# The small transfers of RWKV's block inverse issued on POOL's queue instead of SP's

## Chip, cores and metric

The kernel runs on one core of a Trainium2 chip. The core has five engines with a queue each: TensorE (PE, matrix products into PSUM), VectorE (DVE), ScalarE (ACT), GpSimd (POOL) and SyncE (SP, which only issues transfers). The metric is the device time in microseconds of one execution.

## What is computed

One layer of a hybrid decoder trunk over 512 tokens of width 1,024, in float32: RMSNorm, one input projection, three groups of mixing heads side by side, an output projection with a residual, a gated feed-forward block with a causal convolution, and a last RMSNorm. Cut to what matters:

```python
h = _rmsnorm(x, attn_norm[l])
proj = h @ w_in[l]
p_nsa, p_rw, p_moba = _split(proj, [N_IN_NSA, N_IN_RWKV, N_IN_MOBA])
o_nsa, o_rw, o_moba = ...      # sparse attention | RWKV-7 time mixing | block attention
x = x + concat([o_nsa, o_rw, o_moba]) @ w_out[l]
x = x + _conv_glu(_rmsnorm(x, ffn_norm[l]), ...)
```

The RWKV part is a recurrence over the tokens with a 64 x 64 state for each of four heads:

```python
def step(state, inp):
    r_t, w_t, k_t, v_t, kk_t, a_t = inp
    sa = einsum('bhvk,bhk->bhv', state, -kk_t)
    state = state * w_t[:, :, None, :] + sa[..., None] * (kk_t * a_t)[:, :, None, :] \
            + v_t[..., None] * k_t[:, :, None, :]
    return state, einsum('bhvk,bhk->bhv', state, r_t)
```

## The kernel before

The recurrence is not run token by token. `rw_pair(p, ...)` handles a pair of heads (p = 0, 1) in 8 chunks of 64 tokens. Within a chunk the steps depend on each other through a lower-triangular 64 x 64 matrix, of which the inverse is wanted. It is found in blocks of 16: the 16 x 16 blocks on the diagonal are inverted one by one by elimination, and the rest follows from products on PE (L563 to L575).

The diagonal blocks come out of PE with a token to each partition (`GA`, masked to `NM`, summed to `Nc` at L479: 128 partitions, 8 x 16 numbers each). The elimination on DVE (L491 to L496, fifteen steps of a product and a sum) wants a whole block within a partition (`NB` and `X`: 64 partitions, 256 numbers each). The data is therefore laid out anew through scratch tensors in DRAM, by six transfers of 64 KB for each pair of heads:

- L481 writes `Nc` to `s1`, L483 reads `s1` back as `NB`.
- After the elimination, L503 writes `X`, transposed (`XX`) and as it is, to an `s2` each, and L505 reads each back as `Xc` (named `Nc` in the profile, since it lies in that tile). L508 spreads them to the block-diagonal matrices `DvT` and `Dv`.

A read waits until its write has landed. DVE can't start the elimination before `NB` is there, nor `DvT` and `Dv` before the two reads; PE's L563 needs `DvT`, L571 and L573 need `Dv`. A `lock` lets the second pair start its inverse only after the first pair's.

Beside this run, at the same time, the projections (`proj_fm`, PE's L240 to L242) with weights that SP loads (`wload`, L217, six buffers `wraw`) and that ACT and DVE split into a high and a low part (`whi` L211, `wlo` L212), and the attention heads (`evac_q`: `P` L696, `qt` L701 and L702; scores L784). All of them are generators with hand-written costs that `merge()` interleaves; that gives the order in which instructions are written down. The tile framework then sorts each engine's queue by its own estimate of when an instruction is ready, gives out buffers and sets the semaphores; at run time each queue runs strictly in that order.

Before the change all loads and all these small transfers are issued by SP. POOL clears buffers (L201, L489, L490, L716, L890) and takes a few powers of small tiles (L293, L392, L673, L862, L1455).

Of the kernel before, what the change touches and what calls it, by code (L numbers as in the profile page):

```python
# [78 lines left out]
def cap(name):  # L79
    return CAPS.get(name, CDEF)  # L80
# [11 lines left out]
def hybrid_layer(ctx: ExitStack, tc: tile.TileContext, xT, cst, cols, lora, fgain, wA, wVn, cw1,  # L92
                 wO, wF, wG, out, dbg=None):
    nc = tc.nc
    act, dve, pool, pe, sp = nc.scalar, nc.vector, nc.gpsimd, nc.tensor, nc.sync
# [4 lines left out]
    def at(site):  # L100
        return pool if ENG[site] == 'p' else dve
# [245 lines left out]
    def rw_pair(p, r, k, v, L):  # L347
# [98 lines left out]
        for c0 in (0, 2):  # L446
            yield from want(2)
            pbs = rbank(), rbank()
            for cc in (c0, c0 + 1):
                for j, src in ((0, bb), (1, kb)):  # L450
                    o = ((cc - c0) * 2 + j) * 128
                    for par, cp in ((0, 0), (1, 1), (0, 1), (1, 0)):
                        (r0, r1), (q0, q1) = R64[par], R64[cp]
                        c = 2 * cc + cp
# [3 lines left out]
            for par in range(2):  # L458
                src = pbs[par].rearrange("p (k j a t) -> p a k j t", k=2, j=2, a=2)
# [18 lines left out]
        Nc = v8(NX, 0)  # L478
        dve.tensor_reduce(Nc, NM.rearrange("p (c b j) -> p c j b", b=4, j=16), axis=AX.X, op=OP.add)  # L479
        s1 = dr.tile([NCH, 128, 16], F32, name="s1", bufs=cap("s1"))  # L480
        sp.dma_start(s1.rearrange("c p j -> p c j"), Nc)  # L481
        NB = v16(BT, 0)
        sp.dma_start(NB, s1.rearrange("c (b i) j -> (c b) i j", b=8))  # L483
        for u in range(2):
            dve.tensor_tensor(ch(R)[:, 4 * u:4 * u + 4], GA[u][:, :, :, 0, :].rearrange("p k h t -> p (k h) t"),
                              con("offmask")[:, None, :].to_broadcast([128, 4, CH]), op=OP.mult)
# [13 lines left out]
        Dv, DvT = r2("Dv"), r2("DvT")  # L500
        for src, dst, eng in ((XX, DvT, dve), (X, Dv, at('dv'))):
            s2 = dr.tile([NCH, 128, 16], F32, name="s2", bufs=cap("s2"))
            sp.dma_start(s2.rearrange("c (b i) j -> (c b) i j", b=8), src)  # L503
            Xc = v8(NX, 1 + (src is X))
            sp.dma_start(Xc, s2.rearrange("c p j -> p c j"))  # L505
            for u in range(2):
                c4 = slice(4 * u, 4 * u + 4)
                eng.tensor_tensor(dst.rearrange("p (c b j) -> p c b j", b=4, j=16)[:, c4],  # L508
                                  Xc[:, c4, None, :].to_broadcast([128, 4, 4, 16]),
                                  bsel4, op=OP.mult)  # L510
            yield crw
# [135 lines left out]
        for cc in range(4):  # L647
            for par, cp in ((0, 0), (1, 1), (0, 1), (1, 0)):
                c = 2 * cc + cp
# [533 lines left out]
    def rw_run(p):  # L1183
        g = rw_pair(p, *(rin0 if p == 0 else [rin1[i] for i in (T_R, T_K, T_V)]), L)
        n = 0
        for dt in g:
            yield dt
            n += 1
            mark(f'RW{p}.{n:02d}')
# [362 lines left out]
```

## Time and profile before

| | us |
|---|---|
| three runs | 731.89, 730.33, 729.77 |
| median | 730.33 |
| the profiled execution | 731.48 |
| its span in the profile | 729.4 |

The span runs from the first to the last instruction of the program on the core; the profiled execution's own time has some 2 us around it. In the rows, L12 is line 12 of the kernel; an entry in square brackets is the idle time of the engine ahead of an instruction and what ended it.

### The profile page before, as it was taken

Reading aid. Unit: us, or ns where it says so; the run is one execution under the profiler, and the core shown is the slowest. Engines: PE = TensorE matmul, PEld = TensorE weight load, DVE = VectorE, ACT = ScalarE, POOL = GpSimd, SP = SyncE. Lnnn points to the kernel's source line nnn. Section 1 sums busy time; section 2 is a strip of 40 time slices with the busy share of each in tenths; the row PEclk is TensorE's granted clock in tenths of the full one; section 3 lists DMA queues with packets and bytes.
Section 4 is the critical chain, followed back from the end, with each engine's and each line's share of the span. In section 5 each row is a group of like instructions: output and inputs, shape, how many; then the busy total and the mean of one; then the engine's idle time right before and its main releaser. Section 6 shows DMA issues by size and latency. Waiting matters only on the chain. (4 is left out here: it accounts for less than half of the span.)

```text
span 729.4 us, 13565 instructions
## 1 busy us (share of the span) xinstructions
PE 705.4 (97%) x5156; PEld 613.6 (84%) x5156; DVE 627.0 (86%) x1377; ACT 415.3 (57%) x862; POOL 30.8 (4%) x46
## 2 busy tenths in 40 slices
PE   9999988899999999999999999999999999999995
PEld 6777867678788788888899899999999999998884
DVE  6579679878897999797999999999999999999804
ACT  8475434465656877774766546455564555657403
POOL 4010100000000000011000000000000000000001
PEclk9989989999999999999999999999999999999999
DMA  9622021513110022024246333323333333346003
GB/s 328 193 87 80 13 50 49 140 65 117 44 44 30 1 59 73 30 72 145 74 144 218 97 107 102 116 87 102 97 108 101 102 103 110 98 126 201 1 1 115
DMA packets 44800, 69.86 MB, mean 96 GB/s; under 512 B 10688, under 2 KB 12352, under 8 KB 44736
## 3 DMA queue, kind: packets, MB, share of 16 engines
q1 hardware_dynamic: 44016, 67.95, 29.4%
q10 hardware_dynamic: 720, 1.06, 0.4%
q8 instruction: 40, 0.66, 0.4%
q14 instruction: 24, 0.20, 0.1%
HBM read 64.40 MB, written 4.59 MB: 95 GB/s over the span
## 5 line engine op out<-in xcount | busy, mean ns | idle before, releaser
L1301 ACT CAST ah<-S 128x512 fp32r<-128x512 f32 x88 | 54.5, 621 | 57.6 <-DVE S L1296 57.6
L240 PE MATMUL mm<-xh,whi 128*128 128x512 f32 x152 | 69.6, 458 | 0.0
L241 PE MATMUL acc<-dn,dn 128*128 128x512 f32 (+1 forms) x173 | 64.3, 372 | 0.0
L242 PE MATMUL acc<-dn,dn 128*128 128x512 f32 (+1 forms) x173 | 63.8, 371 | 0.0
L242 PE MATMUL mm<-xh,wlo 128*128 128x512 f32 x152 | 61.8, 406 | 0.0
L241 PE MATMUL mm<-xl,whi 128*128 128x512 f32 x152 | 61.5, 404 | 0.0
L1302 DVE TENSOR_TENSOR al<-S,ah 128x512 fp32r<-128x512 f32 x88 | 58.7, 682 | 0.7 <-ACT ah L1301 0.6
L791 ACT ACTIVATE prob<-prob,fixed 128x128 f32<-128x128 f32 (+1 forms) x72 | 40.5, 563 | 28.5 <-DVE fixed L788 26.5
L240 PE MATMUL acc<-dn,dn 128*128 128x512 f32 (+1 forms) x173 | 54.9, 371 | 0.0
L211 ACT CAST whi<-wraw 128x512 fp32r<-128x512 f32 x70 | 42.6, 618 | 19.8 <-PE mm L241 14.1
L212 DVE TENSOR_TENSOR wlo<-wraw,whi 128x512 fp32r<-128x512 f32 x70 | 47.3, 682 | 3.6 <-PE mm L242 2.2
L240 PE MATMUL pB<-bh,ah 128*128 128x256 f32 x172 | 50.1, 291 | 0.1
L242 PE MATMUL pB<-bh,al 128*128 128x256 f32 x172 | 48.6, 283 | 1.1 <-DVE al L1302 1.0
L242 PE MATMUL pC<-bh,al 128*128 128x256 f32 x172 | 48.5, 282 | 0.3 <-DVE al L1302 0.3
L240 PE MATMUL pC<-bh,ah 128*128 128x256 f32 x172 | 48.5, 282 | 0.2 <-ACT ah L1301 0.2
L241 PE MATMUL pB<-bl,ah 128*128 128x256 f32 x172 | 48.3, 281 | 0.0
L241 PE MATMUL pC<-bl,ah 128*128 128x256 f32 x172 | 48.1, 280 | 0.0
L1302 DVE TENSOR_TENSOR al<-wraw,ah 128x512 fp32r<-128x512 f32 x66 | 43.4, 681 | 0.0
L823 ACT CAST ph<-pt 128x512 fp32r<-128x512 f32 (+3 forms) x72 | 29.7, 425 | 23.3 <-PE pt L816 22.4
L788 DVE CUSTOM_DVE_ANT_0 prob<-s,early 128x128 f32<-128x128 f32 (+1 forms) x72 | 34.7, 483 | 6.6 <-PE s L785 5.0
L1301 ACT CAST ah<-wraw 128x512 fp32r<-128x512 f32 x66 | 36.8, 618 | 1.4 <-DVE x L1135 1.3
L241 PEld LDWEIGHTS acc<-dn,dn 128*128 128x128 f32 x173 | 32.6, 188 | 5.3 <-DVE dn L1365 0.2
(400 smaller groups left out, 2211.8 us busy)
## 6 DMA issues: line engine op xcount, KB each, us to landing
wraw<-in_wF_dram SPq DMA_DIRECT2D x88, 256.0 KB, 2.7
wraw<-in_wG_dram SPq DMA_DIRECT2D x44, 256.0 KB, 3.0
wraw<-in_wA_dram SPq DMA_DIRECT2D x38, 256.0 KB, 3.0
xr<-in_xT_dram SPq DMA_DIRECT2D x16, 256.0 KB, 4.1
wraw<-in_cw_dram SPq DMA_DIRECT2D x16, 256.0 KB, 3.3
wraw<-in_wO_dram SPq DMA_DIRECT2D x16, 256.0 KB, 2.6
fraw<-in_wA_dram SPq DMA_DIRECT2D x8, 256.0 KB, 5.2
x2d<-x2o SPq DMA_DIRECT2D x8, 256.0 KB, 3.3
```

What stands on the lines that cost most here:

```text
L211: act.copy(hi[:, :w], raw)
L212: dve.tensor_tensor(lo[:, :w], raw, hi[:, :w].bitcast(F32), op=OP.subtract)
L240: pe.matmul(o, ah, bh, start=first, stop=False)
L241: pe.matmul(o, ah, bl, start=False, stop=False)
L242: pe.matmul(o, al, bh, start=False, stop=last)
L788: dve.tensor_tensor_reduce(out=P, in0=s_[:, 0:n], in1=con("cmask")[:, 512 - n:512], scale=1.0, scalar=3e38, op0=OP.add, op1=OP.min, accum_ ...
L791: act.activation(P, P, AF.Exp, bias=m, scale=-1.0, accum_out=sums[:, i, par:par + 1])
L823: act.copy(h, t_[:, 0:n])
L1301: act.copy(h, src)
L1302: at(f'L{i}').tensor_tensor(l, src, h.bitcast(F32), op=OP.subtract)
```

## The change

The six transfers of the inverse are issued by POOL (`nc.gpsimd`) instead of SP (`nc.sync`). They move the same bytes between the same places and wait for the same data. POOL has no other transfers.

```diff
@@ -478,9 +478,9 @@
         Nc = v8(NX, 0)
         dve.tensor_reduce(Nc, NM.rearrange("p (c b j) -> p c j b", b=4, j=16), axis=AX.X, op=OP.add)
         s1 = dr.tile([NCH, 128, 16], F32, name="s1", bufs=cap("s1"))
-        sp.dma_start(s1.rearrange("c p j -> p c j"), Nc)
+        pool.dma_start(s1.rearrange("c p j -> p c j"), Nc)
         NB = v16(BT, 0)
-        sp.dma_start(NB, s1.rearrange("c (b i) j -> (c b) i j", b=8))
+        pool.dma_start(NB, s1.rearrange("c (b i) j -> (c b) i j", b=8))
@@ -500,9 +500,9 @@
         Dv, DvT = r2("Dv"), r2("DvT")
         for src, dst, eng in ((XX, DvT, dve), (X, Dv, at('dv'))):
             s2 = dr.tile([NCH, 128, 16], F32, name="s2", bufs=cap("s2"))
-            sp.dma_start(s2.rearrange("c (b i) j -> (c b) i j", b=8), src)
+            pool.dma_start(s2.rearrange("c (b i) j -> (c b) i j", b=8), src)
             Xc = v8(NX, 1 + (src is X))
-            sp.dma_start(Xc, s2.rearrange("c p j -> p c j"))
+            pool.dma_start(Xc, s2.rearrange("c p j -> p c j"))
```

## Rows read from the trace of the kernel before

**Rows 1.** The page's engine totals: busy us, share of the span, instructions.
```profile
PE 705.4 (97%) x5156; PEld 613.6 (84%) x5156; DVE 627.0 (86%) x1377; ACT 415.3 (57%) x862; POOL 30.8 (4%) x46
```

**Rows 2.** Stretches: length, busy us (count) by engine, granted clock, DMA share, GB/s.
```profile
90.00:100.00 10.00, 6.66 (x46) 4.54 (x45) 6.74 (x16) 3.63 (x6) 0.00 (x0) 0.75 0.40 93
```

**Rows 3.** The transfers: packets, and issues with count, KB each, us to landing.
```profile
DMA packets 44800, 69.86 MB, mean 96 GB/s; under 512 B 10688, under 2 KB 12352, under 8 KB 44736
...
Nc<-s SPq DMA_DIRECT2D x4, 64.0 KB, 2.9
...
NB<-s SPq DMA_DIRECT2D x2, 64.0 KB, 2.3
```

**Rows 4.** SP's timeline, 55 to 145 us: start, length, transfer.
```profile
68.14 0.39 SPq L481 DMA_DIRECT2D s<-Nc  x1
...
85.54 1.09 SPq L503 DMA_DIRECT2D s<-X  x2
88.99 1.27 SPq L505 DMA_DIRECT2D Nc<-s  x2
...
110.21 0.47 SPq L483 DMA_DIRECT2D NB<-s  x1
```

**Rows 5.** SP's own waits, 50 to 150 us: total us, times, longest.
```profile
SPq L481 <- DVE Nc L479: 21.9, 2, 13.0
SPq L503 <- DVE X L498: 14.4, 1, 14.4
...
SPq L505 <- DMA s<-X: 3.1, 2, 2.3
```

**Rows 6.** DVE's timeline, 55 to 150 us, around both inverses.
```profile
73.05 0.18 DVE L494 TENSOR_TENSOR NB<-NB,X 64x15 f32<-64x15 f32 x1 [0.18 <-DMA NB<-s]
...
91.50 0.76 DVE L508 TENSOR_TENSOR DvT<-Nc,early 128x256 f32<-128x256 f32 x2 [4.78 <-DMA Nc<-s]
92.58 0.76 DVE L508 TENSOR_TENSOR Dv<-Nc,early 128x256 f32<-128x256 f32 x2 [0.32 <-DMA Nc<-s]
93.25 0.69 DVE L696 SCALAR_TENSOR_TENSOR P<-mm,early 128x512 f32<-128x512 f32 x1
...
114.49 0.17 DVE L494 TENSOR_TENSOR NB<-NB,X 64x15 f32<-64x15 f32 x1
...
140.49 0.76 DVE L508 TENSOR_TENSOR DvT<-Nc,early 128x256 f32<-128x256 f32 x2 [1.37 <-DMA Nc<-s]
```

**Rows 7.** PE's timeline, 84 to 112 us.
```profile
91.37 0.40 PE L242 MATMUL mm<-xh,wlo 128*128 128x512 f32 x1
...
95.91 0.47 PE L784 MATMUL s<-kk,qt 128*128 128x128 f32 x1 [3.34 <-DVE qt L702]
...
97.58 0.79 PE L240 MATMUL mm<-xh,whi 128*128 128x512 f32 x1
...
100.31 0.41 PE L784 MATMUL s<-kk,qt 128*128 128x256 f32 x1
...
105.47 0.39 PE L240 MATMUL mm<-xh,whi 128*128 128x512 f32 x1
...
106.86 0.39 PE L784 MATMUL s<-kk,qt 128*128 128x512 f32 x1
```

**Rows 8.** POOL's timeline, 0 to 260 us.
```profile
1.39 0.52 POOL L716 MEMSET kl<- 64x512 f32 x1
...
30.34 1.02 POOL L293 TENSOR_TENSOR early<-fixed 128x4 f32<-128x4 f32 x1 [11.57 <-DVE fixed L292]
44.87 2.03 POOL L392 TENSOR_TENSOR fixed<-fixed 128x8 f32<-128x8 f32 x1 [13.51 <-DVE fixed L389]
74.02 1.64 POOL L392 TENSOR_TENSOR fixed<-fixed 128x8 f32<-128x8 f32 x1 [27.12 <-DVE fixed L389]
```

**Rows 9.** Waits of PE's weight loads, 55 to 160 us.
```profile
PEld rw L533 <- DVE hl L942: 0.4, 1, 0.4
```

**Rows 10.** Readers and writers of `wraw`, 50 to 150 us: what ended their idle time.
```profile
  PE mm L241: 11.4, 5
```

## The prediction, made before the change was run

> **What bounds the kernel now.** Read the engine totals first [rows 1]: TensorE (PE) is busy for 705.4 of 729.4 us, so nearly every microsecond that PE is made to wait is a microsecond of time, and what PE does not wait for is free. VectorE (DVE) is second at 627.0 us; POOL does almost nothing, 30.8 us. Next, the table by stretches [rows 2]: both block inverses run between 67 and 142 us, and the worst ten microseconds for PE of the whole middle part lie there, 6.66 us busy between 90 and 100 us, with the granted clock at 0.75 on average, so in part at the lower of the two levels (1.2 GHz). Third, the two engines' own timelines. PE stands still for 3.34 us before L784 at 95.91 us, waiting for DVE's `qt` [rows 7]. Going back along DVE [rows 6]: `qt` needs `P` (L696, 93.25 us), which is behind the `Dv` products (92.58), which are behind `DvT` (91.50), which waited 4.78 us for the transfer `Nc<-s` of L505. So one transfer of the moved twelve already sits on the chain that stops PE. The second inverse has the same shape: `DvT` at 140.49 us after a wait of 1.37 us on `Nc<-s`, and a little later PE loads for L533 behind DVE's L942, itself behind `Dv`, after a wait of 0.4 us [rows 9].
>
> **What leaves SP.** Per pair SP issues six transfers: L481, L483, twice L503, twice L505. They cost about 0.4 to 0.5 us of SP each, as 0.39 for one L481 and 1.09 and 1.27 for two L503 and two L505 show [rows 4]; twelve are some 5 us. More time goes where SP stands at them: 21.9 us before L481, 14.4 before L503 [rows 5], and weight loads (L217) stand in line behind. Do the loads come late? In the group of waits on `wraw` from 50 to 150 us, the engines that read it sat idle 11.4 us, and what released them was above all PE (a buffer of the split weights), no transfer [rows 10]. An earlier weight load would land in a buffer that nobody yet wants. I cost the gain at nothing; the cover is the six `wraw` buffers, and if it went, a cast would wait for a landing, about 3 us as for `Nc` (2.9 [rows 3]).
>
> Do the twelve themselves wait behind weight loads on SP? No: SP stands ready at each and waits for what the transfer itself needs, DVE's `Nc` before L481, DVE's `X` before L503, the landed write before L505 (3.1 us) [rows 5]; then it starts them, at 68.14, 85.54 and 88.99 us [rows 4]. So there is no queueing to be saved.
>
> **What is added on POOL.** The shapes decide. L481 and L505 have one side in runs of 16 floats, 64 bytes, so 128x8 = 1,024 pieces for 64 KB; L483 and L503 move 64 runs of 1 KB. Six transfers of 1,024 pieces are 6,144 of the 10,688 packets under 512 B in [rows 3]. SP's landing times show little penalty (2.3 us for `NB`, 2.9 for `Nc` [rows 3]), but the trace holds no transfer issued by POOL. Its cost beyond SP's I bound from POOL's own rows [rows 8]. Low end: nothing, a queue like SP's. High end: POOL's two-operand instruction takes 1.02 us on 128x4 = 512 elements (L293) and 1.64 us on 1,024 (L392); the line through both is 0.40 us fixed and 1.24 us per 1,024. If POOL treats a piece as an element, a 64-piece transfer is later by 0.4 and a 1,024-piece one by 1.64 us. I take 0.4 and 1.0 us: nearer the high end than nothing, because a queue that builds 1,024 pieces in POOL is closer to the row with as many elements than to no work.
>
> The Trainium skill bears on this (DMA: Bandwidth & Descriptors, Specifications): the first byte takes about 1 us from GpSimd and 0.6 from SP or ACT, so 0.4 us per transfer; no row here shows it. By it alone the sum below would be four transfers x 0.4 for the first pair and two x 0.4 for the second, 2.4 us.
>
> **The sum, order of work unchanged.**
> - First pair, `NB`: write (1.0) and read (0.4) later. DVE waits 0.18 us for it at 73.05 already [rows 6], so no slack: +1.4 us, and DVE's chain of L494/L496 ends 1.4 later.
> - First pair, `DvT`/`Dv`: the write L503 +0.4, then two reads one behind the other on POOL, each +1.0, so the second lands 2.4 later. `P` stands behind `Dv`, so PE's gap grows from 3.34 by 1.4 + 2.4 = 3.8 us.
> - Second pair, `NB`: the read is issued at 110.21 and lands 2.3 us on [rows 3, 4], about 112.5; L494 runs at 114.49 [rows 6]. Slack 2.0 covers 1.4: nothing.
> - Second pair, `DvT`/`Dv`: DVE already waits, so +2.4 us, and PE's wait of 0.4 at L533 grows by as much.
> - POOL's other work: `X` of pair 1 is cleared long before it is read, and L392 at 74.02 would come after the read issued near 71: nothing, unless POOL's queue puts a waiting transfer ahead of L392, on whose result DVE's L398 waits next.
>
> Sum 3.8 + 2.4 = 6.2 us. With the high prices: 0.4 + 1.64 + 0.4 + 3.28 = 5.7 and 3.7, 9.4 us. A longer PE gap may also lengthen the slow spell: after the present gap six 128x512 matmuls take 2.73 us (97.58 to the L784 at 100.31), later six take 1.39 (105.47 to the L784 at 106.86) [rows 7], so one more spell costs about 1.3 us; I keep two of them in the upper bound, not in the sum. The profiled execution took 731.48 us (span 729.4 plus 2.1 outside), so it would become 737.7; the median of the runs is 730.33, so I predict 736.5 us. This case's own range is 732.5 (which is past the bound of a measurable change) to 742 (9.4 plus two spells).
>
> **Rivals.**
> - *The transfers are as quick and stay hidden.* POOL's queue could cost no more than SP's. For it: POOL is idle, and none of the four waits in [rows 6] is long but one. Against: DVE waits on three of the four without slack. Time 730.3, within 2.2 us of it (0.3%, about what a measurement of this kernel can tell from no change).
> - *Faster: the order of work changes.* The queues are not in line order: POOL clears `kl` of L716 at 1.39 us, long ahead of L293 [rows 8]. A planner sorts instructions by when it thinks they are ready. If it prices POOL's transfers so that `Nc<-s` comes later than the end of `P`'s matmuls (91.37 + 0.40, about 91.8 us [rows 7]), it will write `P` and `qt` ahead of `DvT`. Then `P` runs about 1.4 us earlier than 93.25, the slow spell (1.3) may go with the gap, and the second pair's wait of 1.37 is filled: -4.1 us, 726.2. It decides when `P` precedes `DvT` in DVE's queue and the later `DvT` is needed by nobody yet. Against: a planner that is off by the same 4.78 us today would have to be right.
> - *Much slower: POOL builds the pieces slowly.* If POOL builds the reading and the writing side of each piece in turn, a 1,024-piece transfer costs 2x1.64 = 3.28 us more. First pair 0.4 + 3.28 + 0.4 + 6.56 = 10.6; second pair 1.6 beyond the slack at `NB` and 7.0 at `Dv`; 19.2 us, 749.5. It becomes the case from about 2 us per transfer. For it: L392 took 2.03 us at 44.87 and 1.64 at 74.02 [rows 8], so POOL's work can be stretched. Against: that is 0.4 us, not a doubling. The Trainium skill has this as a rule against the change (SBUF — State Buffer, SBUF: two separate sides): while DVE runs in a mode that takes both ports, GpSimd can't write its transfer descriptors, and the advice is to issue from ACT or SP; no transfer in the trace of before can show it.
>
> **How the numbers follow.** Chances: order kept and stalls longer 0.43 (736.5); slow building 0.15 (749.5); hidden 0.19 (730.3); reordered for the better 0.23 (726.2). A part of the first case, 0.02, falls within 0.3%. So faster 0.23, same 0.21, slower 0.56. The range leaves out about half of the faster case and half of the slow one, together 0.19: 726.5 to 749 us. The likeliest case alone is 732.5 to 742.
>
> **What the profile after would show.** A new queue of transfers of POOL's, with 12 of 64 KB, and landings longer than 2.3 to 2.9 us: over 3.5 for the 1,024-piece ones if the sum is right, unchanged if they are hidden, over 5 if building is slow. DVE's wait before `DvT` above 4.78 us, `NB`'s above 0.18, and PE's gap before L784 near 7 us. SP no longer standing at L481 and L503, with its weight loads earlier and no cast the better for it. The prediction is wrong if POOL's landings equal SP's, if `P` stands ahead of `DvT`, or if the queues between 150 and 380 us, where PE still waits here and there, are sorted anew: that would move the time by an amount these rows can't price.

## The result, and the profile after

The changed kernel took 735.15 us (median of 6 runs, 734.32 to 737.39); the kernel before, timed beside it, 730.50 (729.77 to 731.89). The ratio is 1.0071, with a 95% interval of 1.0054 to 1.0087: slower by 4.65 us, in the direction of the forecast (736.5) and inside its range. The profiled execution has a span of 733.6 us where the one before had 729.4.

The page's engine totals, the line of packets and the new queue:

```profile
PE 703.9 (96%) x5156; PEld 612.3 (83%) x5156; DVE 627.2 (85%) x1377; ACT 415.7 (57%) x862; POOL 39.8 (5%) x58
...
DMA packets 38464, 69.86 MB, mean 95 GB/s; under 512 B 4544, under 2 KB 5824, under 8 KB 38400
...
q0 software_dynamic: 384, 0.79, 0.5%
...
q8 instruction: 40, 0.66, 0.4%
```

Against [rows 1], POOL has 12 more instructions and 9.0 us more busy time; PE's busy time is 1.5 us less, and the time is longer all the same, so what grew is PE's standing. Against [rows 3], 6,144 small packets are gone: the 12 transfers on POOL's queue make 384 packets, 32 each (the trace's packet records show 16 of 4 KB and 16 of 4 bytes).

The transfers' landings from the same execution (count, KB each, median us), and POOL's timeline, which answers to [rows 4] and [rows 8]:

```profile
s<-X POOLq DMA_DIRECT2D x4, 64.0 KB, 3.2
Nc<-s POOLq DMA_DIRECT2D x4, 64.0 KB, 3.8
...
s<-Nc POOLq DMA_DIRECT2D x2, 64.0 KB, 4.3
NB<-s POOLq DMA_DIRECT2D x2, 64.0 KB, 2.1
```

```profile
67.76 1.07 POOL L481 DMA_DIRECT2D s<-Nc  x1 [21.81 <-DVE Nc L479]
74.10 0.56 POOL L483 DMA_DIRECT2D NB<-s  x1 [5.27 <-ACT vn L747]
76.96 1.66 POOL L392 TENSOR_TENSOR fixed<-fixed 128x8 f32<-128x8 f32 x1 [2.31 <-DVE fixed L389]
88.99 1.12 POOL L503 DMA_DIRECT2D s<-X  x2 [10.37 <-DVE X L498]
91.24 0.93 POOL L505 DMA_DIRECT2D Nc<-s  x1 [1.13 <-DMA s<-X]
93.26 0.90 POOL L505 DMA_DIRECT2D Nc<-s  x1 [1.09 <-DMA s<-X]
...
109.65 0.89 POOL L481 DMA_DIRECT2D s<-Nc  x1 [15.00 <-DVE Nc L479]
112.96 0.55 POOL L483 DMA_DIRECT2D NB<-s  x1 [2.42 <-DMA s<-Nc]
```

The first `s<-Nc` was issued at 67.76 and landed 5.8 us later, the second in 2.8; the view of line L481 gives these two ends of the 4.3 in the list. (At 74.10 the view names ACT's `vn` as the releaser because it ended at about that time; L483 needs the landing.) POOL issues a transfer of 1,024 pieces in 0.9 to 1.07 us and one of 64 runs in 0.55, where SP took about 0.4 to 0.5 [rows 4].

POOL also starts later on what it has waited for. In the second pair the kernel before and then the changed one show:

```profile
106.92 1.03 DVE L479 TENSOR_REDUCE Nc<-NM 128x128 f32<-128x512 f32 x1
107.98 0.38 SPq L481 DMA_DIRECT2D s<-Nc  x1
```

```profile
108.33 1.03 DVE L479 TENSOR_REDUCE Nc<-NM 128x128 f32<-128x512 f32 x1
```

SP issued the write 0.03 us after `Nc` was ready and the read 0.06 after the write's landing; POOL (109.65 and 112.96 above) 0.30 and 0.54 after. From `Nc` to the landing of `NB` it was 4.43 us and is 5.64.

DVE's and PE's timelines and the stretches, against [rows 6], [rows 7] and [rows 2]:

```profile
76.20 0.18 DVE L494 TENSOR_TENSOR NB<-NB,X 64x15 f32<-64x15 f32 x1 [3.98 <-DMA NB<-s]
...
94.23 0.76 DVE L508 TENSOR_TENSOR DvT<-Nc,early 128x256 f32<-128x256 f32 x2 [4.33 <-DMA Nc<-s]
96.61 0.76 DVE L508 TENSOR_TENSOR Dv<-Nc,early 128x256 f32<-128x256 f32 x2 [1.62 <-DMA Nc<-s]
97.28 0.68 DVE L696 SCALAR_TENSOR_TENSOR P<-mm,early 128x512 f32<-128x512 f32 x1
...
144.32 0.76 DVE L508 TENSOR_TENSOR DvT<-Nc,early 128x256 f32<-128x256 f32 x2 [3.26 <-DMA Nc<-s]
145.97 0.76 DVE L508 TENSOR_TENSOR Dv<-Nc,early 128x256 f32<-128x256 f32 x2 [0.89 <-DMA Nc<-s]
```

```profile
76.93 0.39 PE L240 MATMUL mm<-vw,xh 128*128 128x274 f32 x1 [2.95 <-DVE fixed L389]
...
99.94 0.33 PE L784 MATMUL s<-kk,qt 128*128 128x128 f32 x1 [3.23 <-DVE qt L702]
...
100.89 0.50 PE L240 MATMUL mm<-xh,whi 128*128 128x512 f32 x1
...
102.39 0.28 PE L784 MATMUL s<-kk,qt 128*128 128x256 f32 x1
...
144.80 1.15 PE L533 MATMUL rw<-DvT,R 64*64 64x64 f32 x32 [0.90 <-DVE DvT L508]
146.99 0.50 PE L240 MATMUL mm<-xh,whi 128*128 128x512 f32 x1 [1.04 <-DVE Sall L628]
```

```profile
70.00:80.00 10.00, 7.05 (x50) 6.83 (x49) 4.30 (x17) 4.43 (x9) 2.21 (x2) 0.90 0.06 18
80.00:90.00 10.00, 10.00 (x69) 9.43 (x69) 9.52 (x36) 4.16 (x10) 1.01 (x2) 0.93 0.08 26
90.00:100.00 10.00, 6.76 (x72) 4.72 (x70) 4.09 (x9) 3.26 (x7) 2.37 (x5) 1.00 0.28 61
100.00:110.00 10.00, 10.00 (x135) 7.87 (x135) 8.14 (x23) 3.47 (x10) 0.35 (x1) 1.00 0.15 48
```

Three readings. First, PE now stands in two places of the first pair: a new gap of 2.95 us at 76.93, behind L389, which stands behind `NB` in DVE's queue; and the old one before L784, 3.23 us where it was 3.34. Second, in the second pair PE stands 0.90 and 1.04 us around L533, where [rows 9] had 0.4. Third, the granted clock: in the kernel before it was at its lower level behind the gap before L784 (0.75 in [rows 2]); now that stretch has 1.00, six matmuls there take 1.50 us (100.89 to 102.39) where they took 2.73 [rows 7], and the lower level (the trace's clock record puts it from 78.0 to 81.4) falls behind the new gap.

How far the work is behind, from the start times that the views of lines L481 (first and second pair's `s<-Nc`) and L673 (POOL, far behind both inverses) give, in single profiled executions:

```
us                                  L481 to L481    second L481 to L673
before                68.1  108.0   39.9            187.5   79.5
changed               67.8  109.7   41.9            191.0   81.3
L481/L483 on POOL     66.3  107.4   41.1            186.5   79.1
L503/L505 on POOL     66.1  107.0   40.9            188.4   81.4
on ACT's queue        67.0  103.7   36.7            184.3   80.6
SP, P first           67.2  102.8   35.6            182.1   79.3
POOL, P first         66.0  105.2   39.2            185.7   80.5
SP, L508 of pair 1 on POOL   65.6 100.2  34.6       179.7   79.5
SP, L508 of both on POOL     66.8 101.3  34.5       181.9   80.6
changed, packets moved       75.9 114.4  38.5       195.3   80.9
before, packets moved        75.8 112.8  37.0       192.4   79.6
```

The change costs 2.0 us in the first pair's stretch and 1.8 in the second's, 3.8 of the span's 4.2. The other rows are the experiments below.

### The profile page after: what moved, and what is told of

Read it like the earlier page. It is cut to its first block, busy times and chain, and to the rows that moved or that the text cites. A ratio compares the mean times of both kernels' runs of the same rounds, so it can differ in the third digit from the quotient of the medians.

```text
span 733.6 us, 13566 instructions
## 1 busy us (share of the span) xinstructions
PE 703.9 (96%) x5156; PEld 612.3 (83%) x5156; DVE 627.2 (85%) x1377; ACT 415.7 (57%) x862; POOL 39.8 (5%) x58
## 2 busy tenths in 40 slices
DMA packets 38464, 69.86 MB, mean 95 GB/s; under 512 B 4544, under 2 KB 5824, under 8 KB 38400
## 4 chain that ended last, share of the span: by engine, by line
PE 64%; DVE 8%; ACT 4%; issue 1%; DMA 1%; POOL 1%; SPq 0%; POOLq 0%; ACTq 0%
PE acc L241 5%; PE acc L242 5%; PE acc L240 5%; PE mm L240 4%; PE mm L242 4%; PE mm L241 4%; PE pB L240 3%; PE pB L242 3%; PE pB L241 2%; PE ot L804 2%; PE pC L240 2%; PE pC L241 2%; PE pA L241 2%; PE pC L242 2%; PE pA L240 2%; PE pA L242 2%
```

## The experiments

**Which half of the change costs what.** The write and read of `Nc` and `NB` alone on POOL (the lines shown), and, in a second kernel, those of `X` (L503, L505) alone:

```diff
-        sp.dma_start(s1.rearrange("c p j -> p c j"), Nc)
+        pool.dma_start(s1.rearrange("c p j -> p c j"), Nc)
...
-        sp.dma_start(NB, s1.rearrange("c (b i) j -> (c b) i j", b=8))
+        pool.dma_start(NB, s1.rearrange("c (b i) j -> (c b) i j", b=8))
```

> Only L481 and L483 go through POOL; the four transfers of the second half stay on SP. Theory (each longer round trip on POOL's queue stands on DVE's path to the next product, and the two halves add): the first pair's NB is about 3 us later than before, DVE waits some 4 us before L494 at 73 us, P and PE's L784 are about 3 us later; the second pair's NB has slack and costs nothing: 732.5 to 733.5 us against 730.5. Rival (the loss sits in the second half, L503 and L505, or in the sorting of DVE's queue around it): 730.5 within 1 us.

> Only L503 and L505 go through POOL; PE's, DVE's and ACT's queues are in the same order as before, so nothing but the path of the transfers differs. Theory: the second read lands later in both pairs, 1 to 2 us before Dv of the first pair and 2 to 3 us before Dv of the second: 732 to 733.5 us. Rival (the whole loss is the slow first write of the first half, 5.8 us to landing): 730.5 within 1 us. The gains of e1 and e2 over the kernel before should add up to the 4.6 us of the whole change, if nothing is given back.

Measured, with the kernel before at 729.28: 731.75 us, ratio 1.0034 (1.0011 to 1.0056), for the first; 731.46, ratio 1.0031 (1.0019 to 1.0044), for the second. Both times lie under their bands, while the increments, 2.5 and 2.2 us, are those expected (2 to 3 and 1.5 to 3). Their sum, 0.65%, is close to the whole, 0.71%: within these intervals the halves add up. The stretches say where each half costs: the first 1.2 us in the first pair and nothing in the second (39.9 to 41.1, 79.5 to 79.1), the second 1.0 and 1.9. DVE waited 3.10 us for `NB` in the first, where some 4 were expected, and its stretches, of an execution of 730.27 us, show less of the cost than its median does. With L503/L505 alone moved, DVE's timeline of the first pair shows where it waits:

```profile
90.69 0.76 DVE L508 TENSOR_TENSOR DvT<-Nc,early 128x256 f32<-128x256 f32 x2 [6.01 <-DMA Nc<-s]
91.61 0.76 DVE L508 TENSOR_TENSOR Dv<-Nc,early 128x256 f32<-128x256 f32 x2 [0.16 <-DMA Nc<-s]
92.29 0.68 DVE L696 SCALAR_TENSOR_TENSOR P<-mm,early 128x512 f32<-128x512 f32 x1
```

6.01 us against 4.78 [rows 6], and PE's gap before L784 was 4.37 us.

**Is it POOL, or leaving SP?** All twelve on ACT's queue (one of the four lines; the others alike):

```diff
-        sp.dma_start(s1.rearrange("c p j -> p c j"), Nc)
+        act.dma_start(s1.rearrange("c p j -> p c j"), Nc)
```

> All six transfers on ACT's queue, which is of the same kind as SP's, instead of POOL's. Theory (POOL's way of issuing costs, not leaving SP): landings of 2.2 to 3.5 us as on SP, no wait for NB beyond 0.5 us, 730 to 732 us, with whatever ACT loses while it stands at the transfers. Rival (taking them off SP costs or gains by itself, through the weight loads that move up): slower than 734, or faster than 729.

Measured: 727.92 us, ratio 0.9984 (0.9965 to 1.0003): under the 730 to 732 of its theory and past the rival's 729, so the expectation missed. DVE didn't wait for `NB`. With these transfers the planner wrote `P` ahead of `DvT`, the reordering that was a rival in the prediction:

```profile
89.56 0.69 DVE L696 SCALAR_TENSOR_TENSOR P<-mm,early 128x512 f32<-128x512 f32 x1 [2.15 <-PE mm L242]
...
91.25 0.76 DVE L508 TENSOR_TENSOR DvT<-Nc,early 128x256 f32<-128x256 f32 x2
93.47 0.76 DVE L508 TENSOR_TENSOR Dv<-Nc,early 128x256 f32<-128x256 f32 x2 [1.46 <-DMA Nc<-s]
94.27 1.41 DVE L702 TENSOR_TENSOR qt<-P,qt 64x512 fp32r<-64x512 f32 x2
```

PE's gap before L784 fell to 1.72 us. ACT paid for it, though: its L543 stood 2.49 us behind the waiting L505 in its queue. So this run has two differences, and doesn't by itself price the queue; the runs with `P` first, below, put SP's queue and POOL's beside it.

**Why did the first `s<-Nc` take 5.8 us?** Three causes were tried. The first use of POOL's queue, with an extra, unread transfer of the same form, issued at 7.79 us, added to the changed kernel:

```diff
-    dve.memset(idle, 1.0)
+    dve.memset(idle, 1.0); s0 = dr.tile([NCH, 128, 16], F32, name="s0", bufs=1); pool.dma_start(s0.rearrange("c p j -> p c j"), idle[:, 0:128].rearrange("p (c j) -> p c j", j=16))
```

> The changed kernel with one more transfer of the same shape as L481, from a constant tile to a scratch tensor that nobody reads, issued by POOL at about 8 us. Theory 'first use': the 5.8 us to landing of the first L481 are a cost of the queue's first transfer, so the extra one takes it and L481 lands after about 2.8 us as the second pair's did; NB's wait falls from 4.0 to about 1 us and the time to 732 to 733 us. Rival 'busy moment' (what else runs at 68 to 73 us holds it up): L481 still lands after more than 5 us, 735 us.

Measured: 734.94 us, ratio 1.0084 (1.0061 to 1.0106); the first `s<-Nc` still landed in 5.0 us and DVE waited 3.19 for `NB`. That theory falls. Next, also in the changed kernel, a large transfer beside the second `s<-Nc`, because a weight load had been issued on SP 0.3 us behind the first:

```diff
         pool.dma_start(s1.rearrange("c p j -> p c j"), Nc)
+        p and sp.dma_start(dr.tile([128, 512], F32, name="sx", bufs=1), NM)
```

> The changed kernel with one 256 KB write from SP added, of NM, beside the second pair's L481 (its result is read by nobody). Theory A (a large transfer in flight on SP's queue stretches the landing of the 1,024-piece transfer on POOL's): the second pair's s<-Nc lands after more than 4 us, where it was 2.8 in the changed kernel, as the first pair's did (5.8) with a weight load issued 0.3 us behind it. Theory B (the first landing was stretched by DVE being busy, not by the load): the second pair's stays at 2.5 to 3.2 us. The first pair's is 5 to 6 us by both.

Measured: 734.47 us, in a single run. The extra write went out at 106.45 us, a weight load at 106.88 and the second `s<-Nc` at 108.00. Of the transfers of 108 to 112.4 us:

```profile
s<-Nc POOLq DMA_DIRECT2D x1, 64.0 KB, 3.0
```

It landed in 3.0 us, not over 4. But SP's data packets ended at 109.75 us and those of the `s<-Nc` ran from 109.52 to 110.41, while in the first pair the load's ran from 69.05 to 71.15, over the whole of the first fifteen packets (69.93 to 70.65). So this run is a weak test of theory A, and that B's figure came out doesn't show B. The packet records then showed a third cause. The 16 packets of 4 KB of the first `s<-Nc` start as follows, and beside them the one packet of 16 KB that the instruction queue (q8) moved near them:

```
start us             issue   1st     15th    16th    instruction packet
changed              67.76   69.93   70.49   72.07   71.15 to 72.09
L481/L483 on POOL    66.31   68.35   68.94   69.72   68.86 to 69.73
extra transfer       66.11   68.12   68.73   69.63   68.72 to 69.64
POOL, P first        66.00   68.06   68.73   70.05   69.13 to 70.06
load beside          66.14   68.31   68.94   69.89   68.94 to 69.90
changed, 2nd s<-Nc  109.65  111.17  111.40  111.41   none from 107.4 to 117.0
changed, 2nd s<-X    89.58   90.75   90.88   91.87   90.70 to 91.88
```

In all five the sixteenth packet starts within 0.02 us of the end of an instruction packet, 0.8 to 1.6 us behind the fifteenth. One write of `X` in the first pair of the changed kernel (the last row) shows the same. There are 40 such packets on the page for PE's 10,312 matmuls and weight loads, one for each 258, so they were taken for PE's. PE was given thirty narrow matmuls in place of four of its five wide ones to run before its work begins:

```diff
-    for i in range(WARM):
-        pe.matmul(p0[:, 0:256], idle[:, 0:128], idle, start=True, stop=True)
+    for i in [256] * (WARM - 4) + [16] * 30:
+        pe.matmul(p0[:, 0:i], idle[:, 0:128], idle[:, 0:i], start=True, stop=True)
```

> The changed kernel with four of the five idle 128x256 warm-up matmuls of L196 replaced by thirty narrow ones of 16 columns, so that PE runs 26 more small matmuls before it begins; their results are read by nobody. Nothing else differs in any engine's order. Theory C (in the changed kernel the sixteenth of the sixteen 4 KB packets of the first s<-Nc stood behind a 16 KB instruction packet of PE's, which ran from 71.16 to 72.09 us while fifteen packets had started by 70.50): the instruction packets come some 5 to 9 us earlier relative to the work, the first s<-Nc lands in 3.8 to 4.6 us instead of 5.8, DVE's wait for NB falls from 3.98 to 2 to 3 us, and PE's gap of 2.95 us behind L389 to 1 to 2 us. The time is 0 to 2 us less than the changed kernel's, since the narrow matmuls cost PE something at the start. Rival (the late packet is POOL's own: its last pieces are written late, for which DVE's work or the weight load is the reason): the first s<-Nc still lands in 5 us or more, with one packet over 0.8 us behind the others.

Measured: 739.78 us, ratio 1.0147 (1.0121 to 1.0174). The time missed the expectation: the warm-up now lasted to 15.02 us where it had ended at 5.83, and all that follows began some 8 us later. What was asked came out as theory C had it, at the low edge of its figures or just under. The instruction packet ran from 72.31 to 73.59 us, before the issue at 75.94 and 7.0 us earlier against it than in the changed kernel; a weight load was issued at 76.26, as close behind as before; the sixteenth packet started 0.07 us behind the fifteenth:

```profile
wraw<-in_cw_dram SPq DMA_DIRECT2D x1, 256.0 KB, 2.8
s<-Nc POOLq DMA_DIRECT2D x1, 64.0 KB, 3.8
```

```profile
82.38 0.17 DVE L494 TENSOR_TENSOR NB<-NB,X 64x15 f32<-64x15 f32 x1 [1.98 <-DMA NB<-s]
```

```profile
83.11 0.39 PE L240 MATMUL mm<-vw,xh 128*128 128x274 f32 x1 [0.96 <-DVE fixed L389]
...
104.68 0.33 PE L784 MATMUL s<-kk,qt 128*128 128x128 f32 x1 [3.14 <-DVE qt L702]
```

So 2.0 us of the 5.8, and 2.0 of PE's 2.95, were the meeting with an instruction packet; the remaining 3.8 is 1.0 above the second pair's 2.8. As the weight load and DVE's work stood beside it as before, these two can have cost at most that 1.0; which of them did isn't shown. To price the change without the meeting, the same warm-up was put into the kernel before:

> The kernel before, transfers on SP, with the same thirty narrow warm-up matmuls as in the run that moved the instruction packets of the changed kernel (739.78 us, 1.0147 of the kernel before). The difference of the two is what the change costs when no instruction packet meets the first transfer. Theory C (some 2 us of the change's cost is that meeting): the first s<-Nc lands in 2 to 2.5 us, the time is 736.5 to 738.5 us, 1.009 to 1.0125 of the kernel before, so 1.5 to 3 us remain. Rival (the meeting is made up for behind L784 anyway): the time is 734 to 736 us, and the whole 4 to 5 us remain.

Measured: 735.72 us, ratio 1.0093 (1.0070 to 1.0116). Between 1.0147 and 1.0093 lie 0.54%, 3.9 us, against the 0.71% with the meeting. The intervals are too wide to tell the 1.2 us between them from nothing; the time stands in the rival's band and the ratio at the lower edge of theory C's. In the traces the change costs 2.8 us by L673 without the meeting (1.5 and 1.3) and 3.8 with it. But the new warm-up took a meeting from the kernel before, too. There an instruction packet of 86.60 to 87.94 us had stood before the last four of the 64 runs of each `s<-X` of the first pair, which landed in 3.4 and 3.0 us; with the packets moved they landed in 1.9 and 2.0. DVE's wait before `DvT`, 4.78 us in [rows 6], and PE's gap before L784, 3.34 in [rows 7], became:

```profile
97.44 0.76 DVE L508 TENSOR_TENSOR DvT<-Nc,early 128x256 f32<-128x256 f32 x2 [3.19 <-DMA Nc<-s]
```

```profile
101.85 0.33 PE L784 MATMUL s<-kk,qt 128*128 128x128 f32 x1 [1.63 <-DVE qt L702]
```

So about half of the gap that the prediction started from was, by these two executions, a meeting. With the packets moved the first pair's stretch is shorter by 2.9 us in the kernel before and by 3.4 in the changed one. What the meetings add to the price of the change is the difference between the two kernels, about 1 us in these single executions, and not what one meeting costs.

**Does the delay reach PE only because `P` stands behind `Dv`?** The first pair's four L508 products were made to stand behind `P` in DVE's queue, in the kernel before and in the changed one, by an ordering edge alone:

```diff
-                                  bsel4, op=OP.mult)
+                                  bsel4, op=OP.mult); spread[p].append(nc.cur_bb.bb.instructions[-1])
...
-    merge()
+    merge(); [tc.add_manual_dep(i, pins[0].name, mybir.DependencyInfo(mybir.DependencyClass.NoSync, mybir.DependencyReason.DATA), reason="P first") for i in spread[0]]
```

> The kernel before, all twelve transfers on SP, with one change of order: in the first pair the four products of L508 (DvT and Dv) are made to stand behind P (L696) in DVE's queue. Theory 1 (what the transfers' landing costs PE, it costs because P stands behind Dv): PE's gap before L784 shrinks from 3.34 us to about 1.7, as it did with the transfers on ACT's queue where P came first, the slow-clock matmuls behind it (2.73 us for six where 1.39 is the fast figure) may go too, and the time is 1.4 to 3 us under before, about 727 to 729. Rival (the later DvT and Dv are needed at once): the gap only moves to the matmuls that read DvT, and the time is that of before within 0.3%.

> The changed kernel, transfers on POOL, with the same change of order: in the first pair P stands ahead of the four products of L508 in DVE's queue. Theory 1: the late landings of Nc<-s no longer reach PE in the first pair; the gap before L784 falls from 3.23 us to under 2.5, and the time from about 735 to about 731 to 733; what is left is NB's 3 us in the first pair (partly) and the second pair's. Rival: DvT and Dv are needed as soon as P, the gap moves and the time stays at about 735.

Measured, with the kernel before at 729.88: 727.23 us, ratio 0.9962 (0.9945 to 0.9980), with the transfers on SP; 732.62, ratio 1.0044 (1.0026 to 1.0062), with them on POOL. Both moved as theory 1 said. PE's gaps before L784, with SP and then with POOL:

```profile
93.36 0.33 PE L784 MATMUL s<-kk,qt 128*128 128x128 f32 x1 [1.50 <-DVE qt L702]
```

```profile
74.90 0.39 PE L240 MATMUL mm<-vw,xh 128*128 128x274 f32 x1 [2.69 <-DVE fixed L389]
95.51 0.33 PE L784 MATMUL s<-kk,qt 128*128 128x128 f32 x1 [0.85 <-DVE qt L702]
```

With POOL the gap at `NB` stays and hides part of the one before L784.

The answer to the question is no, though: with `P` first on both sides the change still costs 5.4 us (1.0044 against 0.9962), no less than with `P` behind. The late `Nc<-s` of the first pair reached PE through `P`, but the late `NB` reaches it through L389, 2.69 us here and nothing with SP, and the first pair's stretch grows by 3.6 us, the second's by 1.2. ACT's queue, which also had `P` first, lies close to SP's (0.9984): what is dear is POOL's queue, and not leaving SP's.

`qt` still stood behind the products in both, so they were next run by POOL, with the transfers on SP:

```diff
-        for src, dst, eng in ((XX, DvT, dve), (X, Dv, at('dv'))):
+        for src, dst, eng in ((XX, DvT, dve if p else pool), (X, Dv, dve if p else pool)):
```

> The kernel before, transfers on SP, with the first pair's four L508 products run by POOL instead of DVE. Theory 1: P no longer stands behind them, the gap before L784 shrinks from 3.34 us to under 2, but DvT and Dv come some 3 to 6 us later, because POOL takes about 1.6 us for 1,024 elements where DVE takes well under 1; if the matmuls of L533 that read them have that much slack the time is 727 to 729 us, if not it is 731 to 735. Rival: the gap before L784 stays, since DVE is held by something else there.

Measured: 724.60 us, ratio 0.9939 (0.9922 to 0.9957), the fastest of all, below both of its forecasts. PE's gap before L784 was 0.61 us, no stretch between 60 and 120 us fell to the lower clock, and PE stood nowhere over 0.3 us between L784 and 111 us, so POOL's slower products had the slack:

```profile
88.46 1.65 POOL L508 TENSOR_TENSOR DvT<-Nc,early 128x256 f32<-128x256 f32 x2 [8.31 <-DMA Nc<-s]
90.07 2.08 POOL L508 TENSOR_TENSOR Dv<-Nc,early 128x256 f32<-128x256 f32 x2
```

The same for both pairs:

```diff
-        for src, dst, eng in ((XX, DvT, dve), (X, Dv, at('dv'))):
+        for src, dst, eng in ((XX, DvT, pool), (X, Dv, pool)):
```

> The kernel before, transfers on SP, with the four L508 products of both pairs on POOL, where the run with the first pair's alone on POOL took 724.6 us. If the second pair's DvT and Dv have slack at L533, whose wait behind L942 was 0.4 us, L942 and P of the second pair come earlier and the time is 722 to 724 us. If they have none, the products take some 3.7 us on POOL where DVE needs about 1.5, PE waits for DvT or Dv itself, and the time is 725 to 728.

Measured: 727.29 us, ratio 0.9964 (0.9948 to 0.9979), the second outcome: the second pair lacks that slack. Its stretch grew from 79.5 to 80.6 us, and DVE's L628 waited 2.2 us for POOL's `Dv`. The rest of the 2.7 us between the two runs lies outside these stretches and stays open.

## Why the prediction came out right, step by step

- **What bounds it.** Held: what made PE stand before L784 was the chain from `Nc<-s` over `DvT`, `Dv`, `P` and `qt`. The runs that took `P` out of it took 1.8 and 2.7 us of the gap's 3.34 away on SP's queue.
- **SP's gain, nothing.** Held. SP no longer stands at these transfers, and the idle time that readers and writers of `wraw` spend on PE is 10.5 us against 11.4 [rows 10]. ACT's queue gained nothing over SP's either when `P` stood first in both (0.9984 against 0.9962).
- **Price per transfer, 0.4 and 1.0 us.** The sum of a write and a read came out close, 1.2 us (4.43 to 5.64 in the second pair) where 1.4 was forecast, but it is made up otherwise. At each wait POOL started 0.3 to 0.6 us after the release and SP 0.02 to 0.07, a term that the prediction doesn't have. From issue to the first packet a 64-run transfer took 1.26 us on POOL's queue (both `NB`) and 1.26 and 1.31 on SP's: no dearer. One of 1,024 pieces took 1.52 to 1.68 us (the second `s<-Nc`, both `Nc<-s` of the first pair) against 0.91 to 1.05: about 0.6 more. The Trainium skill (DMA: Bandwidth & Descriptors, Specifications) gives GpSimd's first byte 0.4 us more than SP's: the trace agrees for piece-wise transfers, roughly, and not for those of 64 runs.
- **First pair, `NB`, +1.4.** The mis-sized term: DVE waited 3.98 us where it had waited 0.18, so 3.8 more (3.15 by the clock, as this execution stood 0.66 us ahead at L479), since the write met an instruction packet (2.0 us) and, it seems, a weight load. Without the meeting DVE waited 1.98 us where the kernel before with the same warm-up shows no wait, 0.6 more than forecast.
- **First pair, `DvT`/`Dv`, +2.4.** Smaller: from `NB` to `P` the kernel before takes 20.20 us and the changed one 21.08, so 0.9; with the packets moved in both, 18.74 and 19.64, 0.9 again. `s<-X` was no dearer there: without a meeting it landed in 2.0 and 2.1 us on POOL's queue and in 1.9 and 2.0 on SP's, and with the packets not moved both writes had met one on SP's queue, and one of the two on POOL's. `Nc<-s` was dearer by 0.6 (3.1 against 2.5), and the two reads did not add up, since each started on the landing of its own write.
- **Second pair, `NB`, nothing.** Held: L494 ran at 115.92 without a wait.
- **Second pair, `DvT`/`Dv`, +2.4.** Held: from the second L481 to `P` (142.85 before, 147.18 after) it is 2.7 us more, of which 1.8 remain by L673. The parts differ from the forecast, though: `Nc<-s` there landed in 4.7 us against 3.3 (4.5 and 2.7 with the packets moved), `s<-X` in 3.2 against 2.5. SP, which had held its weight loads back at L503 and L505, now issues them beside (eight loads from 129.08 us on). That they stretch the landings is argued from this, not tried.
- **PE's gap near 7 us, failed in form.** It was 3.23, as PE had already stood 2.95 us for `NB`. The two make 6.2 where 3.34 + 3.8 = 7.1 was forecast.
- **The slow spell.** It was kept as an extra cost; it turned into a gain. The lower clock lasted from 95.1 to 101.9 us before and from 78.0 to 81.4 after, so the first pair lost 2.0 us by the second L481 although `P` came 4.4 later counted from the first (25.1 to 29.5).
- **Sum.** 6.2 forecast (3.8 + 2.4), 3.8 by L673 and 4.2 of span measured: the first pair's half was the one oversized, at 2.0. That it came so near is in part luck. At `P` the first pair was 4.4 us behind where 3.8 was forecast, from 3.5 for `NB` instead of 1.4 and 0.9 for `DvT`/`Dv` instead of 2.4, and 2.4 us of it came back behind L784, which no term had foreseen.
- **Rivals and signs.** Hidden: no, DVE's waits grew for `NB` (0.18 to 3.98) and `Dv` (0.32 to 1.62). The one before `DvT`, forecast above 4.78 us, was 4.33, as the first `s<-X` met no packet now. Slow building: no, issues of 0.9 to 1.07 us are far from 2 us or more extra, and the late landing followed an instruction packet. The Trainium skill's rule that DVE in its two-port mode keeps GpSimd from writing descriptors (SBUF — State Buffer, SBUF: two separate sides) had, at the first `s<-Nc`, at most 1.0 us to show itself in: with the packet out of the way the first `s<-Nc` landed in 3.8 us beside the same DVE work, and the second pair's in 2.8. No run here shows whether DVE was in that mode then. Reordering: not in this kernel, but a real mechanism, worth 2.7 us as an edge; with the products on POOL besides, 5.3.

## What to carry to other kernels

Before moving a small transfer to an idle engine's queue, find the instruction that waits for it and what stands behind that one in its engine's queue, and count what the new queue adds at each wait: here 0.3 to 0.6 us from a release to the issue, and 0.6 more to the first packet of a piece-wise transfer. Taking `P` out from behind the wait was worth 2.7 us with every transfer left on SP. The idle engine was better used for the waiting instructions themselves (0.9939) than for their transfers (1.0071). And give a landing on a short chain a margin for what shares the transfer engines: instruction packets, and perhaps weight loads that the old queue had held back.

## What the runs showed of the hardware that was not expected

- A 64 KB transfer in 1,024 pieces of 64 bytes appears as 1,024 packets on SP's queue and as 16 of 4 KB and 16 of 4 bytes on POOL's.
- A 16 KB instruction packet of 0.88 to 0.96 us held one of sixteen packets of a transfer back by 0.8 to 1.6 us in five runs. In the kernel before, SP's 1,024 packets started from 69.06 to 69.86 us and the instruction packet at 69.89: it had missed them by little. It was not free of meetings: four of the 64 runs of each `s<-X` of its first pair started at 87.93 us or later, behind a packet that ended at 87.94.
- POOL issued each transfer that it had stood waiting for 0.28 to 0.63 us after what it waited for (`Nc`, `X` or a landing) was there, SP 0.02 to 0.07, in all runs.
- From the end of the held-back packet (72.52 us) to the landing (73.54) passed 1.02 us; behind the last packet of `NB` (75.81) 0.37. What the rest was stays open.
- Gaps of 3.1 to 3.3 us of PE before L784 were followed by the lower clock in the kernel before and with L481/L483 on POOL, and not in the changed kernel, with or without its packets moved. In the kernel before with its packets moved a gap of 1.63 us was followed by it (103.6 to 107.0 us).
